# Five matmuls for a K tile instead of six, softplus on VectorE, and first casts in a written order

## The chip, the cores and the metric

The kernel runs on one core of a Trainium2 chip. The metric is the time of one execution on the device in microseconds (us). Before the change it is 855.6 us, the median of three runs (855.42, 855.6 and 856.59). In the profile, PE is TensorE's matmul, PEld its weight load, DVE is VectorE, ACT is ScalarE, POOL is GpSimd, SP is SyncE, which issues most DMAs. L85 is line 85 of the kernel.

## The reference, cut to what matters

One layer for 512 prompt tokens and 64 sample tokens, which share the weights: together T = 576 tokens, D_MODEL = 1024, D_FF = 2816, all in float32.

```python
h = rmsnorm(x, norm_mix)
proj = einsum('bld,de->ble', h, w_in)        # columns for three groups of heads
# A, gated DeltaNet, 4 heads: conv + SiLU on q, k, v; chunks of 64 rows
g = -exp(a_log) * softplus(aa + a_dt_bias)
beta = sigmoid(ab)
o_a, new_delta = gated_delta_rule(q, k, v, g, beta, delta_s0)
# B, differential attention, 4 heads; C, trailing means of 4 channel groups
x = x + einsum('ble,ed->bld', concatenate([o_a, o_b, o_c]), w_out)
u = einsum('bld,df->blf', rmsnorm(x, norm_ffn), w_up)
gate, val = split_cols(causal_dwconv(u, buf, w_conv, b_conv), (D_FF, D_FF))
x = x + einsum('blf,fd->bld', silu(gate) * val, w_down)
y = rmsnorm(x, norm_final)
```

## The kernel before

Activations lie transposed: 128 channels on the partitions, 576 tokens along the free axis, so a product of 1024 channels has 8 K tiles of 128. To keep float32's accuracy on faster fp32r matmuls, weights and activations are split into a high part, rounded to fp32r, and a low part, the rest. A K tile of a product is wh·xh + wh·xl + wl·xh, and each of the three goes in two matmuls, over the tokens 0 to 255 and 256 to 575 (`PARTS`): six matmuls, each with its own weight load, 1728 columns.

`gemm` (L190) makes one tile of 128 output channels in a PSUM tile `g` of 1024 columns (two banks), of which there are two. The tokens lie in its columns 256 to 831, so that the first part ends one bank and the second begins the other; columns 0 to 255 are unused. `accumulate` does a share of the K tiles of such a product. Each product takes its weights from `weights`: one 128x1024 slab at a time is loaded by SP (`w_raw`), cast on ACT (L174, `w_hi`) and subtracted on VectorE (L175, `w_lo`), two buffers each, so the next slab's cast waits until TensorE has read the buffer of the one before.

The order of the work on TensorE is written out: `mm` and `transpose` keep their instructions in program order and move a clock on by the columns at 2.4 GHz. Side work (the chains of the heads, the decay, the convolutions, the transposes of the result) are generators; `spawn` and `yield n` write their next matmuls n ns of that clock later, between the K tiles of the running product. On VectorE, ACT and POOL a scheduler sets the order. The program computes, in this order: the first two tiles of w_in together with the split of x (L340 to L368); 30 more tiles of w_in, beside which the delta rule and the attention run; w_out in 8 tiles, first 8 K tiles of each (the sum goes to DRAM, `x1_d`), then the other 4, which need the last heads of the attention (L1190 to L1202; the sum is read back as `w`, and the first two tiles of this part have their products begun early); ffn_up in 44 tiles, each with conv, SiLU and product; ffn_down in 8 tiles of 22 K tiles, whose sum `xr` (L1259) is transposed by TensorE (L89) and normed. The last tile of ffn_down has its own loop (`last_weights`, L1176).

The decay (`gates`) needs softplus: a chain of small operations of 128x20 elements, of which 17 run on POOL and the others on VectorE (L474 to L489), then `gt`, which four small matmuls read (they are written 11000 ns after the chain is issued).

Of the kernel before, what the change touches and what calls it, by code (L numbers as in the profile page):

```python
# [26 lines left out]
PARTS = (slice(0, CUT), slice(CUT, T))  # L27
O0 = 512 - CUT
# [31 lines left out]
def hybrid_step(ctx: ExitStack, tc: tile.TileContext, I, O):  # L60
# [69 lines left out]
    def act_tile():  # L130
        return act.tile([P, T], F32R, name="a", bufs=NSLOT)
# [60 lines left out]

    def gemm(xs):
        ps = psg.tile([P, 1024], F32, name="g")
        n = 3 * len(xs)
        i = 0
        xs = iter(xs)
        while i < n:
            for wh, wl in weights():
                xh, xl = next(xs)  # L200
                for w, x in ((wh, xh), (wh, xl), (wl, xh)):
                    for r in PARTS:
                        mm(ps[:, O0:O1][:, r], w, x[:, r], start=i == 0, stop=i == n - 1)
# [56 lines left out]
    def col(nm, i):  # L260
        return par[:, off[nm] + i:off[nm] + i + 1]
# [10 lines left out]
    def wide_pair():  # L272
        return [act.tile([P, KT, T], F32R, name="wide", bufs=2) for _ in range(2)]

    hmix_hi, hmix_lo = wide_pair()
    hmix = [(hmix_hi[:, k], hmix_lo[:, k]) for k in range(KT)]

# [23 lines left out]
    load_first(nc.scalar, slice(0, 2))  # L301
    load_first(nc.sync, slice(2, 8))
# [32 lines left out]
    def first_products():  # L335
# [1017 lines left out]
```

## Time and profile before

| | before |
|---|---|
| median of three runs | 855.6 us |
| the profiled execution | 856.47 us |
| its span, first to last instruction | 854.7 us |
| PE busy | 835.0 us (98%), 6350 matmuls |
| VectorE busy | 534.3 us (63%) |
| ACT busy | 357.3 us (42%) |
| POOL busy | 116.1 us (14%) |
| mean granted clock of TensorE | 0.991 |

The profiled execution is 0.9 us over the median, and 1.8 us of it lie outside the span. A share of busy time is a mean over stages that have different limits, so it only tells where to look; a wait of TensorE is told by the engine and line that released it. Where operations on one line are pipelined, the distance from one start to the next tells their cost, not their listed length.

### The profile page before, as it was taken

The page shows a single profiled execution, that of the slowest core. Times are in us where ns is not written, and L with a number is a line of the kernel's source. Part 1 is how long each engine was busy: PE and PEld are TensorE (multiplying, and loading weights), DVE is VectorE, ACT ScalarE, POOL GpSimd, SP SyncE. Part 2 cuts the span into 40 slices and gives each one's busy share as a digit, 9 for nine tenths or more (in the row PEclk, how much of TensorE's full clock was granted, in tenths as well). Part 3 has the DMA queues.
Part 4 walks back from the last instruction along what each step waited for, and adds up shares of the span by engine and source line. Part 5 has one row for each costly group of instructions (what it writes and reads, how often), then busy time and mean ns, then how long its engine had stood idle before and what let it go on. Part 6 is the DMA issues. An engine that isn't in the chain of part 4 may idle for free.

```text
span 854.7 us, 15955 instructions
## 1 busy us (share of the span) xinstructions
PE 835.0 (98%) x6350; PEld 809.0 (95%) x6350; DVE 534.3 (63%) x1189; ACT 357.3 (42%) x789; POOL 116.1 (14%) x183
## 2 busy tenths in 40 slices
PE   9969999999999999999999999999999999999996
PEld 8969999999999888889999999999999999999996
DVE  7748876884347677774867767667667673323422
ACT  6336563144444455552544344343343442222322
POOL 3332310210002000000012112112121120000001
PEclk9989999999999999999999999999999999999998
DMA  6232222242113432425822222222222223333413
GB/s 245 75 100 78 79 79 77 94 123 77 41 60 94 162 102 67 131 81 170 293 72 78 90 84 75 99 76 80 93 76 97 77 69 111 86 103 86 122 58 111
DMA packets 39033, 84.83 MB, mean 99 GB/s; under 512 B 9387, under 2 KB 14527, under 8 KB 38959
## 3 DMA queue, kind: packets, MB, share of 16 engines
q1 hardware_dynamic: 37870, 82.31, 30.1%
q10 hardware_dynamic: 1088, 1.51, 0.5%
q8 instruction: 50, 0.82, 0.4%
q14 instruction: 25, 0.20, 0.1%
HBM read 72.98 MB, written 10.82 MB: 98 GB/s over the span
## 4 chain that ended last, share of the span: by engine, by line
PE 89%; DVE 4%; DMA 2%; ACT 2%; POOL 1%; issue 1%; POOLq 0%; SPq 0%; DVEq 0%; ACTq 0%
PE g L85 75%; PE m L85 11%; PE m L89 3%; DVE w_lo L175 1%; DMA XT<-gsum_d 1%; ACT w_hi L174 0%; DMA inv<-kq 0%; DMA w<-x_d 0%; DMA x<-in_xT_dram 0%; POOL t L484 0%; POOL t L483 0%; POOL osc L267 0%; DVE oatt L991 0%; DMA Xc<-inv 0%; DVE stat L950 0%
## 5 line engine op out<-in xcount | busy, mean ns | idle before, releaser
L85 PE MATMUL g<-wide,w_hi 128*128 128x256 f32 x1472 | 267.4, 302 | 0.9 <-ACT w_hi L342 0.6
L85 PE MATMUL g<-t,w_hi 128*128 128x256 f32 (+1 forms) x1408 | 242.7, 294 | 0.0
L85 PEld LDWEIGHTS g<-wide,w_hi 128*128 128x128 f32 x1472 | 224.0, 191 | 4.6 <-issue 1.3
L85 PEld LDWEIGHTS g<-t,w_hi 128*128 128x128 f32 x1408 | 210.2, 188 | 0.0
L174 ACT CAST w_hi<-w_raw 128x1024 fp32r<-128x1024 f32 (+2 forms) x109 | 110.6, 1016 | 169.2 <-PE g L85 158.8
L85 PE MATMUL g<-wide,w_lo 128*128 128x256 f32 x736 | 161.7, 302 | 0.2 <-DVE w_lo L343 0.2
L175 DVE TENSOR_TENSOR w_lo<-w_raw,w_hi 128x1024 fp32r<-128x1024 f32 (+2 forms) x109 | 128.2, 1177 | 46.5 <-ACT w_hi L174 45.2
L85 PE MATMUL g<-t,w_lo 128*128 128x256 f32 x704 | 150.4, 295 | 0.0
L85 PEld LDWEIGHTS g<-wide,w_lo 128*128 128x128 f32 x736 | 124.2, 191 | 2.3 <-issue 0.9
L85 PEld LDWEIGHTS g<-t,w_lo 128*128 128x128 f32 x704 | 117.4, 188 | 0.1
L1215 POOL COPY fout<-u 128x4 f32<-128x4 f32 x44 | 51.2, 1164 | 223.1 <-DVE u L1206 223.1
L1212 DVE SCALAR_TENSOR_TENSOR c<-u,par,c 128x511 f32<-128x511 f32 (+3 forms) x176 | 78.9, 511 | 2.5 <-ACT c L1208 2.5
L1206 DVE TENSOR_TENSOR u<-g,rstd 128x576 f32<-128x576 f32 x44 | 33.3, 758 | 59.8 <-PE g L85 58.3
L85 PE MATMUL g<-w,w_hi 128*128 128x256 f32 (+1 forms) x280 | 48.4, 295 | 0.0
L85 PEld LDWEIGHTS g<-w,w_hi 128*128 128x128 f32 x280 | 42.0, 188 | 0.0
L1208 ACT ACTIVATE c<-u,par 128x576 f32<-128x576 f32 x44 | 38.3, 870 | 4.2 <-DVE u L1206 1.4
L1232 ACT ACTIVATE s<-c 128x576 f32<-128x576 f32 x22 | 15.1, 687 | 46.0 <-DVE c L1214 46.0
L267 POOL TENSOR_TENSOR osc<-sso,mhalf 128x5 f32<-128x5 f32 x8 | 9.4, 1182 | 179.6 <-DVE sso L772 62.3
L85 PE MATMUL g<-w,w_lo 128*128 128x256 f32 (+1 forms) x140 | 29.9, 294 | 0.0
L1143 ACT ACTIVATE junk<-m 128x128 f32<-128x128 f32 (+1 forms) x40 | 10.9, 274 | 43.7 <-PE m L89 35.3
L1144 DVE TENSOR_TENSOR t<-m,nf 128x128 f32<-128x128 f32 (+1 forms) x40 | 11.2, 289 | 23.7 <-ACT junk L1143 23.7
L85 PE MATMUL g<-kq,w_hi 128*128 128x256 f32 (+1 forms) x128 | 23.4, 301 | 0.0
(314 smaller groups left out, 1026.3 us busy)
## 6 DMA issues: line engine op xcount, KB each, us to landing
w_raw<-in_ffn_up_dram SPq DMA_DIRECT2D x44, 512.0 KB, 3.2
w_raw<-in_w_in_dram SPq DMA_DIRECT2D x30, 512.0 KB, 3.3
w_raw<-in_ffn_down_dram SPq DMA_DIRECT2D x16, 512.0 KB, 3.5
w_raw<-in_w_out_dram SPq DMA_DIRECT2D x8, 512.0 KB, 3.6
w_raw<-in_ffn_down_dram SPq DMA_DIRECT2D x8, 384.0 KB, 3.2
xr<-in_xT_dram SPq DMA_DIRECT2D x8, 288.0 KB, 3.5
x_d<-xr SPq DMA_DIRECT2D x8, 288.0 KB, 2.1
w<-x_d SPq DMA_DIRECT2D x8, 288.0 KB, 5.8
```

The source lines that it names most:

```text
L85: ordered(nc.tensor.matmul(out, lhsT=lhsT, rhs=rhs, start=start, stop=stop), n / 2.4 if rhs.dtype == F32R else max(54, n / 0.6))
L89: ordered(nc.tensor.transpose(out=out, in_=in_, identity=identity), 107)
L174: nc.scalar.copy(hi[:, :kt], raw)
L175: last_split[0] = nc.vector.tensor_sub(lo[:, :kt], raw, hi[:, :kt].bitcast(F32)).ins
L267: nc.gpsimd.tensor_tensor(out, x, epst[:x.shape[0], :x.shape[1]], op=ALU.pow)
L1143: nc.scalar.activation(junk[:n], src, AF.Square, scale=D ** -0.5, accum_out=op["part"][:n, c, m:m + 1])
L1144: nc.vector.tensor_mul(op["yt"][c][m // 4][:n, (m % 4) * P:(m % 4 + 1) * P], src, op["nf"][:n, m * P:(m + 1) * P])
L1206: nc.vector.tensor_mul(u, ps[:, O0:O1], rstd)
L1208: nc.scalar.activation(c, u, AF.Identity, scale=fw[:, 2, t:t + 1], bias=col("ffn_conv_b", t))
L1212: nc.vector.scalar_tensor_tensor(c[:, a + d:b], u[:, a:b - d], fw[:, j, t:t + 1], c[:, a + d:b], op0=ALU.mult, op1=ALU.add)
L1215: nc.gpsimd.tensor_copy(fout[:, :, :, t], u[:, NP - 64:].rearrange("p (s c) -> p s c", c=64)[:, :, 62:])
L1232: nc.scalar.activation(s, cv[0], AF.Silu)
```

## The change

A K tile becomes five matmuls. The high and the low part of an activation now lie in one tile, so that the 256 first tokens of both can stream through the same high weight at once: 512 columns, high part into the columns 256 to 511 of `g` as before, low part into the columns 0 to 255. `fold` adds the two when a product is complete: a copy to SBUF on ACT, an addition on VectorE. The tiles of activations become pairs (`act_pair`, `wide_pairs`, `t_pair`, `wide_slot`); the last tile of ffn_down keeps its six matmuls.

The softplus series runs on VectorE alone, and its matmuls are written 6500 ns after it instead of 11000. Three other delays grow. At the start, ACT's casts, activations and squares are kept in a written order, and the squares of a pair of channels come one step later.

```diff
+    def k_tile(ps, w, x, start=False, stop=False):
+        (wh, wl), (xh, xl, xb) = w, x
+        mm(ps[:, :2 * CUT].rearrange("p (a t) -> p a t", a=2), wh, xb, start=start, stop=False)
+        yield False
+        mm(ps[:, O0:O1][:, REST], wh, xh[:, REST], start=start, stop=False)
+        mm(ps[:, O0:O1][:, REST], wh, xl[:, REST], start=False, stop=False)
+        yield False
+        mm(ps[:, O0:O1][:, REST], wl, xh[:, REST], start=False, stop=stop)
+        mm(ps[:, O0:O1][:, HEAD], wl, xh[:, HEAD], start=False, stop=stop)
+        yield False
+
+    def fold(ps):
+        low = act.tile([P, CUT], F32, name="low", bufs=2)
+        nc.scalar.copy(low, ps[:, :CUT])
+        nc.vector.tensor_add(ps[:, O0:O1][:, HEAD], ps[:, O0:O1][:, HEAD], low)
+
     def gemm(xs):
         ps = psg.tile([P, 1024], F32, name="g")
-        n = 3 * len(xs)
         i = 0
-        xs = iter(xs)
-        while i < n:
-            for wh, wl in weights():
-                xh, xl = next(xs)
-                for w, x in ((wh, xh), (wh, xl), (wl, xh)):
-                    for r in PARTS:
-                        mm(ps[:, O0:O1][:, r], w, x[:, r], start=i == 0, stop=i == n - 1)
-                    i += 1
-                    yield False
+        while i < len(xs):
+            for w in weights():
+                yield from k_tile(ps, w, xs[i], i == 0, i == len(xs) - 1)
+                i += 1
+        fold(ps)
         return ps
...
+    nc.scalar.copy(epst[:, :1], epst[:, :1])
...
+        for j in range(KT // 2):
+            for k in (2 * j, 2 * j + 1):
...
+                tc.keep_in_program_order(nc.scalar.activation(hi, x, AF.Identity, scale=col("norm_mix", k)))
...
+                if k < 2:
+                    split_first((slice(0, 2), slice(2, 8))[k])
+                for w in range(2):
+                    for _ in k_tile(ps[w], (his[w][:, k], los[w][:, k]), hmix[k], k == 0, k == KT - 1):
+                        pass
+            if j:
+                add_squares(j - 1)
+        add_squares(KT // 2 - 1)
+        for p in ps:
+            fold(p)
...
-        nc.gpsimd.tensor_scalar_add(t2, t1, 2.0)
+        nc.vector.tensor_scalar_add(t2, t1, 2.0)
         nc.vector.reciprocal(t2, t2)
-        nc.gpsimd.tensor_mul(z, t1, t2)
-        nc.gpsimd.tensor_mul(z2, z, z)
-        nc.vector.tensor_scalar(t1, z2, 1.0 / 17, 1.0 / 15, op0=ALU.mult, op1=ALU.add)
-        for d in (13, 11, 9, 7, 5, 3, 1):
-            nc.gpsimd.tensor_mul(t1, t1, z2)
-            nc.gpsimd.tensor_scalar_add(t1, t1, 1.0 / d)
-        nc.vector.scalar_tensor_tensor(t1, t1, 2.0, z, op0=ALU.mult, op1=ALU.mult)
+        nc.vector.tensor_mul(z, t1, t2)
+        nc.vector.tensor_mul(z2, z, z)
+        nc.vector.tensor_scalar_mul(t1, z2, 1.0 / 17)
+        for d in (15, 13, 11, 9, 7, 5, 3):
+            nc.vector.scalar_tensor_tensor(t1, t1, 1.0 / d, z2, op0=ALU.add, op1=ALU.mult)
+        nc.vector.tensor_scalar(t1, t1, 1.0, 2.0, op0=ALU.add, op1=ALU.mult)
+        nc.vector.tensor_mul(t1, t1, z)
...
-        yield 11000
+        yield 6500
...
-            yield 1530
+            yield 2600
...
-            yield 1070
+            yield 1900
...
-                yield 400 + nk
+                yield 1000 + nk
```

On VectorE, before, around the softplus (`t_468` and `z` are its tiles, `tmp`, `vT` and `kq` belong to heads, `gt` is what TensorE waits for):

```order
L481 TENSOR_SCALAR t_468<-z_471 128x20
L175 TENSOR_TENSOR w_lo<-w_raw,w_hi 128x1024
L540 SCALAR_TENSOR_TENSOR vT<-tmp,ah,vT 128x579 x3
L545 SCALAR_TENSOR_TENSOR vT<-tmp,vT 128x579
L485 SCALAR_TENSOR_TENSOR t_468<-t_468,z 128x20
L535 TENSOR_TENSOR tmp<-g,rstd_129 128x512
L536 TENSOR_TENSOR tmp<-g,rstd_129 128x64
L486 SCALAR_TENSOR_TENSOR t_468<-y,t_468 128x20
L175 TENSOR_TENSOR w_lo<-w_raw,w_hi 128x1024
L489 SCALAR_TENSOR_TENSOR gt<-t_468,ea 128x20
L540 SCALAR_TENSOR_TENSOR kq<-tmp,ah,kq 128x579
L492 MEMSET gt 64x4
```

and after, where `t_454` is the series:

```order
L180 TENSOR_TENSOR w_lo<-w_raw,w_hi 128x1024
L498 TENSOR_SCALAR t_454<-z_457 128x20
L214 TENSOR_TENSOR g<-g,low 128x256
L500 SCALAR_TENSOR_TENSOR t_454<-t_454,z_457 128x20
L552 TENSOR_TENSOR tmp<-g,rstd_130 128x512
L553 TENSOR_TENSOR tmp<-g,rstd_130 128x64
L500 SCALAR_TENSOR_TENSOR t_454<-t_454,z_457 128x20 x5
L557 SCALAR_TENSOR_TENSOR vT<-tmp,ah,vT 128x579
L500 SCALAR_TENSOR_TENSOR t_454<-t_454,z_457 128x20
L557 SCALAR_TENSOR_TENSOR vT<-tmp,ah,vT 128x579
L501 TENSOR_SCALAR t_454<-t_454 128x20
L557 SCALAR_TENSOR_TENSOR vT<-tmp,ah,vT 128x579
```

The series now stands on VectorE itself, between one `w_lo`, a fold and the head's products; the second `w_lo` no longer stands before `gt`. On TensorE the `gt` matmuls stood behind K tile 32 and now stand behind K tile 30.

On VectorE, before, where the second part of w_out begins (the last `xr` of the first part, then the running sums `w`):

```order
L1099 TENSOR_TENSOR xr<-xr,g 128x576
L175 TENSOR_TENSOR w_lo<-w_raw,w_hi 128x512
L1131 MEMSET r_5141 128x5
L1252 MEMSET part 128x40
L1193 TENSOR_TENSOR w_4809<-w_4809,g 128x576
L1193 TENSOR_TENSOR w_4825<-w_4825,g 128x576
```

and after:

```order
L180 TENSOR_TENSOR w_lo<-w_raw,w_hi 128x512
L214 TENSOR_TENSOR g<-g,low 128x256
L1119 TENSOR_TENSOR xr<-xr,g 128x576
L1154 MEMSET r_4897 128x5
L1270 MEMSET part 128x40
L214 TENSOR_TENSOR g<-g,low 128x256
L1218 TENSOR_TENSOR w_4593<-w_4593,g 128x576
L214 TENSOR_TENSOR g<-g,low 128x256
L1218 TENSOR_TENSOR w_4593<-w_4593,g 128x576
```

`xr` has moved behind a `w_lo` and a fold, and each sum `w` behind a fold of its own.

On VectorE, before, at the end of one tile of ffn_down (`xr` is its sum, `t` the normed result after the transposes):

```order
L175 TENSOR_TENSOR w_lo<-w_raw,w_hi 128x768
L175 TENSOR_TENSOR w_lo<-w_raw,w_hi 128x1024
L1259 TENSOR_TENSOR xr<-xr,g 128x576
L175 TENSOR_TENSOR w_lo<-w_raw,w_hi 128x1024
L1144 TENSOR_TENSOR t<-m,nf 128x128 x4
L1144 TENSOR_TENSOR t<-m,nf 64x128
```

and after:

```order
L180 TENSOR_TENSOR w_lo<-w_raw,w_hi 128x768
L180 TENSOR_TENSOR w_lo<-w_raw,w_hi 128x1024 x2
L214 TENSOR_TENSOR g<-g,low 128x256
L1277 TENSOR_TENSOR xr<-xr,g 128x576
L1167 TENSOR_TENSOR t<-m,nf 128x128 x4
L1167 TENSOR_TENSOR t<-m,nf 64x128
```

The sum `xr` has moved behind the second `w_lo` of 1024 and a fold. On TensorE the transposes of `xr` stand as many K tiles behind the end of the product as before.

## Rows read from the trace of the kernel before

**Rows 1.** The page, busy us, share of the span and instructions of TensorE.

```profile
PE 835.0 (98%) x6350; PEld 809.0 (95%) x6350; DVE 534.3 (63%) x1189; ACT 357.3 (42%) x789; POOL 116.1 (14%) x183
```

**Rows 2.** TensorE's waits: line, releaser, us in total, times, longest.

```profile
PE m L85 <- ACT wt L970: 1.2, 3, 0.4
...
PE m L85 <- DVE Y L679: 0.8, 1, 0.8
```

**Rows 3.** Timeline of all engines around the decay, idle time and releaser in brackets.

```profile
37.57 1.05 ACT L174 CAST w_hi<-w_raw 128x1024 fp32r<-128x1024 f32 x1 [1.18 <-PE g L85]
...
37.84 0.69 DVE L535 TENSOR_TENSOR tmp<-g,rstd 128x512 f32<-128x512 f32 x1 [0.44 <-PE g L85]
...
39.79 2.53 DVE L540 SCALAR_TENSOR_TENSOR vT<-tmp,ah,vT 128x579 f32<-128x579 f32 x3
...
46.41 0.26 POOL L484 TENSOR_SCALAR t<-t 128x20 f32<-128x20 f32 x1
...
46.70 0.18 DVE L485 SCALAR_TENSOR_TENSOR t<-t,z 128x20 f32<-128x20 f32 x1 [2.78 <-POOL t L484]
...
49.92 1.01 PE L85 MATMUL m<-gt,cst 128*128 128x20 f32 x4 [5.73 <-DVE gt L492]
...
51.84 1.33 PE L85 MATMUL g<-wide,w_hi 128*128 128x256 f32 x4
```

**Rows 4.** Busy us by engine, TensorE's clock, DMA share, GB/s of a stretch.

```profile
191.22:194.63 3.41, 3.41 (x21) 3.13 (x20) 3.14 (x8) 2.87 (x10) 0.00 (x0) 0.52 0.00 0
```

**Rows 5.** TensorE's timeline in ffn_up: start, us, line, operation, tiles, count.

```profile
600.05 0.69 PE L85 MATMUL g<-t,w_hi 128*128 128x256 f32 x4
...
601.63 0.28 PE L85 MATMUL g<-t,w_hi 128*128 128x256 f32 x1
```

**Rows 6.** TensorE's timeline in the last ffn_down tile, same columns.

```profile
832.06 1.92 PE L85 MATMUL m<-wide,u 128*128 128x320 f32 x12
833.83 4.56 PE L85 MATMUL m<-w,t 128*128 128x320 f32 x30
838.22 1.34 PE L85 MATMUL m<-a,s 128*128 128x256 f32 x10
...
839.97 1.56 PE L85 MATMUL m<-wide,c 128*128 128x256 f32 x12
841.37 1.33 PE L85 MATMUL m<-wide,u 128*128 128x256 f32 x10
```

**Rows 7.** Timeline of VectorE in ffn_down, same columns.

```profile
738.56 1.23 DVE L175 TENSOR_TENSOR w_lo<-w_raw,w_hi 128x1024 fp32r<-128x1024 f32 x1
```

**Rows 8.** Timeline of ACT at the end of the first products.

```profile
21.12 1.99 ACT L174 CAST w_hi<-w_raw 128x1024 fp32r<-128x1024 f32 x2 [1.53 <-PE g L85]
```

**Rows 9.** Groups by line and shape: busy us, mean ns, idle before (ACT).

```profile
L927 ACT COPY wts<-m 128x256 f32<-128x256 f32 x4 | 1.5, 372 | 2.3 <-PE m L85 2.3
```

**Rows 10.** The same groups of VectorE.

```profile
L603 DVE SCALAR_TENSOR_TENSOR U<-m,w,tq 128x256 f32<-128x256 f32 x16 | 7.5, 478 | 0.9 <-PE m L85 0.7
...
L343 DVE TENSOR_TENSOR w_lo<-w_raw,w_hi 128x256 fp32r<-128x256 f32 x2 | 0.8, 418 | 0.0
```

**Rows 11.** Timeline where the second half of w_out begins.

```profile
395.13 0.62 ACT L174 CAST w_hi<-w_raw 128x512 fp32r<-128x512 f32 x1 [2.74 <-issue]
...
395.35 0.76 DVE L1099 TENSOR_TENSOR xr<-xr,g 128x576 f32<-128x576 f32 x1 [2.19 <-PE g L85]
...
401.92 0.80 PE L85 MATMUL g<-wide,w_hi 128*128 128x256 f32 x4 [0.21 <-DVE w L1193]
```

**Rows 12.** Groups of VectorE there, 402 to 422 us.

```profile
L1198 DVE SCALAR_TENSOR_TENSOR t<-w,par,t 128x576 fp32r<-128x576 f32 x7 | 5.7, 816 | 0.7 <-ACT t L1197 0.7
L1193 DVE TENSOR_TENSOR w<-w,g 128x576 f32<-128x576 f32 x7 | 5.3, 751 | 0.5 <-DMA w<-x_d 0.2
...
L175 DVE TENSOR_TENSOR w_lo<-w_raw,w_hi 128x512 fp32r<-128x512 f32 x4 | 2.7, 686 | 1.3 <-ACT w_hi L174 1.3
```

**Rows 13.** Timeline of TensorE in ffn_down.

```profile
740.48 0.71 PE L89 MATMUL m<-cst,xr 128*128 128x128 f32 x5
```

More of the change, by code (lines that the diff above doesn't have):

```diff
@@ L27 @@
 PARTS = (slice(0, CUT), slice(CUT, T))
+HEAD, REST = PARTS
 O0 = 512 - CUT
@@ L270, in hybrid_step, with wide_pairs @@
     x2_d = dram.tile([P, KT, T], F32, name="x2_d")
[L272 to L276, printed above, removed]
+    def wide_pairs():
+        tiles = [act.tile([P, KT // 2, 2, T], F32R, name="wide", bufs=2) for _ in range(2)]
+        return [split_pair(t[:, k]) for t in tiles for k in range(KT // 2)]
+    hmix = wide_pairs()
     abstack = ExitStack()
@@ L614, in hybrid_step @@
         last_inv = [None]
+        rows_pair = []
         def invert():
             n = 80
-            rows = [act_tile().bitcast(F32)[:n, :512] for _ in range(2)]
+            rows = [rows_pair[0][:n, i, :512] for i in range(2)]
             xb_f = kq_tile().rearrange("p i t -> p (i t)")[:n]
@@ L857, in attn_proj @@
             else:
-                dst = [act_tile().bitcast(F32) for _ in range(2)]
+                pair = act_pair().bitcast(F32)
+                dst = [pair[:, 0], pair[:, 1]]
             for i in range(3):
@@ L1036, in own_weight @@
             nc.sync.dma_start(raw, src)
-            hi, lo = (act_tile()[:, :512].rearrange("p (k m) -> p k m", m=P) for _ in range(2))
+            pair = act_pair()
+            hi, lo = (pair[:, i, :512].rearrange("p (k m) -> p k m", m=P) for i in range(2))
             nc.scalar.copy(hi, raw)
@@ L1073, in projections @@
             yield from after("windows")
-            his, los = wide_pair()
-            for i in range(8):
-                mixed[4 + i] = his[:, i], los[:, i]
+            mixed.update(zip(range(4, 12), wide_pairs()))
             yield from after("delta")
@@ L1164, in last_weights @@
         def last_weights():
-            tags = [("t", 16)] * 6 + [("u", 2)] * 2 + [("c", 3)] * 2 + [("s", 2)] * 2
+            halves = [t[:, i] for t in (t_pair(), t_pair(), t_pair()) for i in range(2)]
+            halves += [fp.tile([P, T], F32R, name=nm, bufs=bufs) for nm, bufs in (("u", 2), ("c", 3), ("s", 2)) for _ in range(2)]
             ws = []
@@ L1173, in last_weights @@
                     n = min(4, kt - b)
-                    hi, lo = (fp.tile([P, T], F32R, name=nm, bufs=bufs)[:, :n * P].rearrange("p (k m) -> p k m", m=P)
-                              for nm, bufs in (tags.pop(), tags.pop()))
+                    hi, lo = (halves.pop()[:, :n * P].rearrange("p (k m) -> p k m", m=P) for _ in range(2))
                     nc.scalar.copy(hi, raw[:, b:b + n])
@@ L1247, in feed_forward @@
             nc.sync.dma_start(op["nf"], I["norm_final"].partition_broadcast(P))
-            op["yt"] = [[fp.tile([P, T], F32R, name="t", bufs=16).bitcast(F32)[:, :512] for _ in range(2)]
-                        for c in range(5)]
+            op["yt"] = [[t[:, i, :512] for i in range(2)] for t in (t_pair().bitcast(F32) for c in range(5))]
             op["part"] = fin.tile([P, 5, KT], F32, name="part")
```

93 lines of the change are left out of this document (40 added, 53 removed).

## The prediction, made before the changed kernel had run

> **What bounds the kernel now.** I read the page's busy times first: TensorE is busy 98% of the span [rows 1]. The end is therefore set by how long the matrix products take and by the few places where TensorE stands still. The second view is TensorE's own waits: the reader is to see how small they are, 1.2 us in 3 for `wt` and 0.8 us for `Y` [rows 2], beside a single large one of 5.73 us for the decay `gt`, which the timeline shows in its place [rows 3]. The third is a table of stretches, for the granted clock: it fell to 0.52, about 1.2 GHz, from 191.22 on, in the 3.41 us behind a stretch in which TensorE had waited for `Y` [rows 4]. Last come the products themselves, in TensorE's timeline.
>
> **Five matmuls for six.** A K tile takes (601.63 - 600.05)/2 = 0.79 us [rows 5]. It streams 3 x (256 + 320) = 1728 columns, at 2.4 GHz 0.72 us; 70 ns are over, or 11.7 ns per matmul. After the change it streams the same 1728 columns in five matmuls: two of 256 become one of 512, so one weight load and one matmul's excess go. No matmul of 512 columns of this kind stands in the trace. The nearest rows are runs of one shape near the end: 12 of 320 columns take 833.83 - 832.06, 147.5 ns each (14.2 over 320/2.4); 30 of 320 take 146.3 ns (13.0 over); 12 of 256 take 841.37 - 839.97, 116.7 ns (10.0 over) [rows 6]. If the excess belongs to the matmul, 512 columns take 213.3 + 10.0 to 14.2 = 223.3 to 227.5 ns against 2 x 116.7 = 233.4, a gain of 5.9 to 10.1 ns. If it belongs to the columns, 512 take 233.4 and nothing is gained; a straight line through 116.7 and 147.5 gives even 239.9, a loss of 6.5 ns. I take the excess of the longest run of the shape nearest to 512, 13.0 ns: 226.3 ns, gain 7.1 ns. There are 858 K tiles (w_in 256, w_out 96, ffn_up 352, ffn_down 7 x 22 = 154; the last ffn_down tile keeps its six). 858 x 7.1 ns = **-6.1 us** (ends +5.6 and -8.7). TensorE waits for nothing in those stretches, so this is on the path. VectorE, ACT and the weight DMAs have as much to do per gemm as before, in 8 x 7 ns less, apart from the fold below.
>
> The Trainium skill (TensorE: Matmul & The Clock Gate, "Wait — 56ns, not 53.3ns?") speaks against part of this gain: it says that back to back a matmul costs its columns at 2.4 GHz plus a fixed part of about 2.5 ns. By it one matmul less per K tile saves 858 x 2.5 = 2.1 us instead of 6.1, and the sum below would be 4.0 us higher. The rows do not agree on the total (10 to 14 ns over, not 2.5), but they do not show how much of it is fixed.
>
> **Softplus on VectorE.** Before, TensorE reaches the `gt` matmuls at 49.92 - 5.73 = 44.19 and stands until 49.92; the POOL series of 14 operations ends only at 46.41 + 0.26, and VectorE then still has `tmp`, a `w_lo` and `gt` itself to do [rows 3]. After, the gt matmuls are written behind K tile 30 instead of 32, so TensorE comes 2 x 0.79 = 1.6 us earlier, at about 42.6. The order on VectorE puts a `w_lo` into the chain whose cast ends at 37.57 + 1.05 = 38.62 [rows 3]; from there: `w_lo` 1.23 [rows 7], a fold 0.42, `tmp` 0.69 and its small second part, about 0.9 together, three `vT` products 2.53 [rows 3], and 13 small operations of 20 columns or fewer (up to 0.18 each [rows 3]) about 2.0: 38.6 + 1.2 + 0.4 + 0.9 + 2.5 + 2.0, about 45.6. TensorE waits some 3.1 to 3.4 us instead of 5.73: -2.4. Behind the old wait four matmuls took 1.33 us instead of 0.69, at half clock [rows 3, 5]; about two K tiles ran so, 1.6 to 1.9 us. A wait of 3 us may bring that again; I count a quarter of it as won, -0.4. Together **-2.8 us** (0 if chain and clock stay; -7.6 if both go). The series leaves POOL; nobody then waits for POOL here but the next `cout` copies, which are not on the path. VectorE's new small operations stand before products `kq`, whose reader is the ACT and then the transposes; the wait for `kt` behind them I leave as it is.
>
> **Longer delays** (front tokens 2600, levels 1900, values 1000 + nk). They write the waiting matmuls later among K tiles that need nothing: the `wt` waits (1.2) and the `Y` wait (0.8) go [rows 2], and with the latter perhaps the half clock: 3.41 us at 0.52 did work of 1.77 us [rows 4], so 1.6 us hang on it; I count half. **-2.8 us** (-1 to -3.7). What is late next is the end of the inversion's six levels, which then comes later by 6 x 0.8 us; the head work that waits for it has gemms of other heads beside it.
>
> **Start.** The first products are bound by the hi and lo parts, as before. In VectorE's new order the last `total` addition stands behind the `w_lo` of the third weight, whose cast waits for the first buffers, that is for TensorE's K tile 16; before, it ran at 21.12 to 23.11 with the next one [rows 8] and nothing of the sums stood behind it. The first products end about 1 us sooner, the sums start about 2 us later than they could: **+0.7 us** (-1 to +3).
>
> **The fold.** Each of the 99 gemms gets an ACT copy 128x256 out of PSUM and a VectorE addition 128x256 in PSUM before its result can be read. Nearest rows: ACT 372 ns; VectorE 418 ns without and 478 ns with PSUM [rows 9, 10]; I take 0.37 and 0.42. In most stages the gemm's result is used several us before anyone needs it, and 99 x 0.42 = 42 us of VectorE lie beside TensorE. In three places they don't.
>
> First, the second half of w_out (8 gemms of 4 K tiles). Before, the last `xr` addition starts at 395.35 and the x1 store and loads follow it; TensorE has products of the first two tiles to do meanwhile and then meets its data 0.21 us late, at 401.92 [rows 11]. After, VectorE's order has `w_lo` (whose cast ends at 395.13 + 0.62), fold and then `xr`: 395.75 + 0.69 + 0.42 + 0.76 = 397.6 instead of 396.1, +1.5 us with no cover. From there each gemm gives VectorE 0.82 + 0.75 + 0.69 and a squares addition like the second, 3.0 us [rows 12], against 4 x 0.79 = 3.16 of TensorE; with 0.42 it is 3.4 against 3.13, and two PSUM buffers tie one to the other: 7 x 0.29 = 2.0. **+3.5 us** (1 to 5).
>
> Second, ffn_down. The transposes of `xr` stand 3.67 K tiles (2.9 us) behind the gemm's end in both orders, since their delay of 2500 is kept. Before, VectorE added `xr` at once, while ACT still cast, then did `w_lo` at 738.56, when the cast had ended; the transposes came at 740.48, with no wait [rows 7, 13]. After, the order is `w_lo`, fold, `xr`: 738.56 + 1.23 + 0.42 + 0.76 = 740.97, that is 0.65 us after the transposes' weight load is due at about 740.34. Five tiles at 0.65 and one, where the last weights' splits stand there too, at 1.5: **+4.8 us** (2 to 6). ffn_up has the same order, but its reader comes a whole gemm later.
>
> Third, the heads' chains, queued behind `w_lo` and fold: **+0.5 us** (0 to 4).
>
> **Sum.** -6.1 - 2.8 - 2.8 + 0.7 + 3.5 + 4.8 + 0.5 = -2.2 us. The profiled execution took 856.47 us, its span 854.7 and 1.8 around it; so 852.5 and 854.3. The median of the three runs is 855.6, 0.9 under the profiled one, and on its scale I forecast **853.4 us**.
>
> **Rivals.**
> (A) The excess is per column. For it: the excess grows from 10.0 to 14.2 when the columns grow by a quarter [rows 6]. Against: it grows by less between 256 and the run of 30. The gain of 6.1 is then nothing: 859.5, slower. It decides from 512 columns taking over about 231 ns. The Trainium skill's small fixed part (the section above) leads to the same side, with 857.4.
> (B) VectorE's place in the order decides: `w_lo`, fold and `xr` end more than 2.9 us behind a gemm's end, and each 0.1 us over that costs 0.1 in six ffn_down tiles and about as much in seven w_out gemms. If the ACT copy, queued behind a cast, and the addition come in a row (0.8 instead of 0.42), it is 6 x 0.4 + 7 x 0.6 = +6.6: 860.0, slower. For it: ACT's order has the copy behind the next cast. Against: that cast ends before `w_lo` does, so the copy is done when VectorE comes to it.
> (C) The waits go wholly: no gt wait and no half clock (-7.6 instead of -2.8), and in ffn_down VectorE takes 2.0 instead of 4.8. 853.4 - 4.8 - 2.8 = 845.8. For it: 13 small operations are short on VectorE. Against: `w_lo` and fold stand among them.
> (D) The change does not do this part: `gt` is as late as before against its matmuls and the clock falls again. 853.4 + 2.8 = 856.2.
>
> **Chances.** What a measurement of this kernel can tell from no change is about 0.2%, 1.7 us: faster is under 853.9, slower over 857.3. Forecast 0.42 (own range 849 to 857.5): of it 0.27 faster, 0.11 same, 0.04 slower. A 0.20: 0.03, 0.05, 0.12. B 0.12: 0, 0.02, 0.10. C 0.16: all faster. D 0.10: 0.02, 0.06, 0.02. Together 0.48, 0.24, 0.28. The range goes from C to just over B, 845 to 861; what it leaves out is A with a loss per matmul (865) and C with more.
>
> **What would show it.** Pitch of a K tile in ffn_up: 0.783 us if right, 0.79 with A, 0.78 or under with a larger gain. The `gt` wait about 3.3 us and at 42 us instead of 44. TensorE waits for `xr` in six ffn_down tiles, 0.6 each; none would make me wrong by 4.8. A TensorE wait of over 1 us at the start of w_out's second half. Waits for `wt` and `Y` gone. Wrong altogether: the five matmuls slower than six, or waits that I have nowhere, as for folds in ffn_up.

## The result, and the profile after

The changed kernel takes 888.6 us (median of 4 runs, 887.9 to 890.1) against 856.1 us: ratio 1.038, 95% interval 1.036 to 1.040. The forecast was 853.4 us, so it is 35 us off and on the wrong side, outside the range of 845 to 861. The profiled execution took 888.5 us with a span of 886.7, 32.0 more than before.

The page of the changed kernel first: busy us of the engines, and TensorE's granted clock in 40 slices, in tenths of full speed.

```profile
PE 845.2 (95%) x5492; PEld 775.3 (87%) x5492; DVE 569.0 (64%) x1299; ACT 378.6 (43%) x889; POOL 52.1 (6%) x166
...
PEclk9999999999999999789999999999999999999998
```

Line numbers are those of the changed kernel (`mm` is L86 there, the cast L179, `w_lo` L180, the fold L213 and L214). TensorE has 858 matmuls fewer than in [rows 1], one per K tile, and is busy 10 us longer; it stands still for 41.5 us instead of 19.7. Slices 17 and 18 (354 to 399 us) have a clock of 0.7 and 0.8. The waits of TensorE are the second view (line, releaser, us in total, times, longest):

```profile
PE m L90 <- DVE p L978: 4.5, 3, 2.6
PE m L90 <- DVE xr L1277: 3.1, 6, 1.3
PE m L86 <- DVE gt L509: 3.0, 1, 3.0
PE m L86 <- DVE wide L1018: 2.7, 2, 1.4
PE m L90 <- DVE m L967: 2.4, 2, 1.6
PE g L86 <- DVE w L1218: 2.3, 3, 1.0
PE m L90 <- ACT p L972: 2.0, 1, 2.0
PE m L86 <- DVE total L367: 2.0, 1, 2.0
```

`wt` and `Y` of [rows 2] are gone. `gt` has fallen from 5.73 to 3.0 us, and the stretch at half clock that comes with it, by the granted clock, from 6.8 to 3.4 us. In their place stand `p`, `m` and `wide`: they belong to the softmax and the output of the attention, which had 0.5 us of such waits before, and the prediction had 0.5 us for them. `xr` (ffn_down), `w` (w_out's second part) and `total` (the start) are the ones it named.

To see where the 32.0 us are, I counted the columns of the products in both traces; the time at which the same K tile begins can then be compared, whatever stands between. Each row is the change of the time of a stretch:

| K tiles | what runs there | before | after | change |
|---|---|---|---|---|
| to 16 | start, first two products | 29.8 | 31.9 | +2.2 |
| 16 to 64 | w_in, decay (`gt`) | 55.9 | 51.2 | -4.7 |
| 64 to 128 | w_in, fronts of the heads | 60.0 | 62.9 | +2.9 |
| 128 to 256 | w_in, inversion, delta rule | 152.1 | 152.3 | +0.2 |
| 256 to 304 | first part of w_out, attention | 82.4 | 107.4 | +25.0 |
| 304 to 352 | rest of it, second part | 41.1 | 44.5 | +3.4 |
| 352 to 704 | ffn_up | 280.7 | 280.3 | -0.4 |
| 704 to the end | ffn_down, output | 152.7 | 156.2 | +3.4 |

**The products.** In ffn_up nothing but the products decides. TensorE's timeline of the changed kernel, with single matmuls' starts (start, us, engine, line, operation, tiles, count):

```profile
600.45 0.40 PE L86 MATMUL g<-t,w_hi 128*128 128x512 f32 x1
...
600.68 0.46 PE L86 MATMUL g<-t,w_hi 128*128 128x320 f32 x2
...
600.98 0.43 PE L86 MATMUL g<-t,w_lo 128*128 128x320 f32 x2
...
601.24 0.39 PE L86 MATMUL g<-t,w_hi 128*128 128x512 f32 x1
```

The 512 columns take 600.68 - 600.45 = 0.23 us, the two of 320 take 0.30, the 320 and the 256 take 0.26: 0.79 us again, as in [rows 5]. Over all K tiles from 600 to 700 us the distance from a matmul of 512 to the next is 230.9 ns on average; two of 256 took 2 x 116.7 = 233.4 in [rows 6], 2.5 ns more. ffn_up's 352 K tiles gained 0.4 us, 1.1 ns each. The rate is not the same everywhere: K tiles 128 to 176, where TensorE ran nothing but products, took 38.40 us before and 38.08 after, 6.7 ns less per K tile.

**The attention.** The busy times of the heads' stretches, two before (first fence) and three after (busy us of PE, PEld, DVE, ACT, POOL with counts, then TensorE's clock, DMA share, GB/s):

```profile
313.00:328.00 15.00, 14.59 (x106) 12.11 (x105) 10.47 (x37) 8.72 (x25) 0.00 (x0) 1.00 0.22 75
340.00:354.00 14.00, 14.00 (x105) 12.03 (x105) 10.00 (x33) 7.88 (x24) 0.00 (x0) 1.00 0.24 82
```

```profile
317.00:338.00 21.00, 17.73 (x95) 14.02 (x94) 12.05 (x41) 8.95 (x29) 1.17 (x1) 0.84 0.17 54
351.00:372.00 21.00, 18.06 (x93) 14.76 (x92) 11.34 (x38) 7.61 (x23) 0.00 (x0) 0.76 0.16 53
386.00:406.00 20.00, 17.82 (x97) 14.17 (x96) 12.23 (x42) 8.87 (x26) 0.19 (x1) 0.83 0.18 57
```

No engine is near its limit after. TensorE stands idle 3.3, 2.9 and 2.2 us in the three stretches, and in each of them the clock is at 1.2 GHz for part of the time: 0.84, 0.76 and 0.83 on average, that is 2 x (1 - 0.84) x 21 = 6.7 us, 10.1 and 6.8 us at half clock. At full clock the work of these 23.6 us takes half, so 11.8 us go with the clock. TensorE's waits in the whole attention sum up to 13.1 us (1.7 before). 13.1 - 1.7 + 11.8 = 23.2 of the 25.0.

Here is the first of the stretches, with a piece of the head before it, in TensorE's timeline of the changed kernel:

```profile
299.31 1.09 PE L86 MATMUL m<-cv,wts 128*64 128x128 f32 x8
...
316.19 1.13 PE L86 MATMUL m<-kq 64*128 64x512 f32 x4
...
322.45 1.33 PE L86 MATMUL m<-ew,pr 128*128 128x64 f32 x10 [1.25 <-DVE ew L936]
...
325.02 0.66 PE L90 MATMUL m<-cst,p 128*128 128x128 f32 x4
327.69 0.92 PE L90 MATMUL m<-cst,oatt 128*128 128x128 f32 x5 [2.02 <-ACT p L972]
328.54 1.97 PE L86 MATMUL m<-cv,wts 128*64 128x128 f32 x8
...
332.78 1.31 PE L86 MATMUL g<-wide,w_hi 128*128 128x512 f32 x3
```

The widest scores (`m<-kq`, 64x512) run at 316.19. TensorE then waits 1.25 us for `ew`, and 2.02 us at 327.69, where a PSUM bank is freed by the exponentials of the next scores. Behind that the eight matmuls `m<-cv,wts` take 1.97 us, where the same eight took 1.09 us for the head before, at 299.31: the clock has fallen. What VectorE did between the scores and their maximum, in the changed kernel:

```profile
317.11 1.23 DVE L180 TENSOR_TENSOR w_lo<-w_raw,w_hi 128x1024 fp32r<-128x1024 f32 x1 [1.16 <-ACT w_hi L179]
...
318.38 0.45 DVE L214 TENSOR_TENSOR g<-g,low 128x256 f32<-128x256 f32 x1
...
318.83 0.62 DVE L968 TENSOR_REDUCE stat<-m 128x1 f32<-128x512 f32 x1
...
319.43 0.74 DVE L1119 TENSOR_TENSOR xr<-xr,g 128x576 f32<-128x576 f32 x1
320.10 0.68 DVE L968 TENSOR_REDUCE stat<-m 128x1 f32<-128x512 f32 x1
...
320.77 1.04 DVE L1009 TENSOR_SCALAR oatt<-oatt,osc 128x128 f32<-128x128 f32 x5
321.73 0.22 DVE L969 TENSOR_SCALAR stat<-stat,qneg 128x2 f32<-128x2 f32 x1
...
322.05 0.26 DVE L936 TENSOR_SCALAR ew<-cst,mx 128x64 f32<-128x64 f32 x1
```

VectorE idles 1.16 us for a cast, because `w_lo` stands first; then come a fold, one maximum (`stat`), `xr`, the other maximum, the five `oatt`. The scaled maximum, for which the exponentials wait, is ready at 321.73 + 0.22 = 321.95, 5.8 us after the scores began. Before, the order was the maxima and `xr` first and `w_lo` behind them (both engines' timeline of the kernel before):

```profile
310.08 1.13 PE L85 MATMUL m<-kq 64*128 64x512 f32 x4
...
312.29 0.67 DVE L950 TENSOR_REDUCE stat<-m 128x1 f32<-128x512 f32 x1
...
313.88 0.75 DVE L1099 TENSOR_TENSOR xr<-xr,g 128x576 f32<-128x576 f32 x1
314.54 0.23 DVE L951 TENSOR_SCALAR stat<-stat,qneg 128x2 f32<-128x2 f32 x1
314.67 1.22 DVE L175 TENSOR_TENSOR w_lo<-w_raw,w_hi 128x1024 fp32r<-128x1024 f32 x1
```

There it took 314.77 - 310.08 = 4.7 us. For the next head the scaled maximum of the changed kernel is ready at 356.44 + 0.21 = 356.65, 6.8 us after the scores, and TensorE waits for `m`, and later for `p`, both from VectorE:

```profile
349.89 1.13 PE L86 MATMUL m<-a 64*128 64x512 f32 x4
...
356.44 0.21 DVE L969 TENSOR_SCALAR stat<-stat,qneg 128x2 f32<-128x2 f32 x1
...
360.37 1.09 PE L90 MATMUL m<-cst,p 128*128 128x128 f32 x4 [1.59 <-DVE m L967]
...
380.63 0.30 PE L90 MATMUL m<-cst,p 128*128 128x128 f32 x1 [2.60 <-DVE p L978]
```

In the order on TensorE the widest scores of heads 1 to 3 stood at K tiles 262, 278 and 294 before and stand at 264, 280 and 296 after. All these products have 8 K tiles and begin at multiples of 8, so the scores have moved to the very place where a product ends and `w_lo`, fold and `xr` come due.

### The profile page after: what moved, and what is told of

It is laid out like the page before. It is cut to its first block, busy times and chain, and to the rows that moved or that the text cites. A ratio compares the mean times of both kernels' runs of the same rounds, so it can differ in the third digit from the quotient of the medians.

```text
span 886.7 us, 14467 instructions
## 1 busy us (share of the span) xinstructions
PE 845.2 (95%) x5492; PEld 775.3 (87%) x5492; DVE 569.0 (64%) x1299; ACT 378.6 (43%) x889; POOL 52.1 (6%) x166
## 4 chain that ended last, share of the span: by engine, by line
PE 81%; DVE 9%; ACT 4%; DMA 3%; issue 2%; ACTq 0%; POOLq 0%; SPq 0%; DVEq 0%
PE g L86 67%; PE m L86 12%; PE m L90 2%; DVE w_lo L180 2%; ACT w_hi L179 2%; DVE stat L968 1%; DMA w_raw<-in_ffn_down_dram 1%; DVE g L214 1%; ACT p L972 1%; DMA w_raw<-in_w_out_dram 1%; DMA w_raw<-in_w_in_dram 1%; DMA XT<-gsum_d 1%; DVE xr L1277 1%; DMA inv<-kq 0%; DVE w L1218 0%
## 5 line engine op out<-in xcount | busy, mean ns | idle before, releaser
L86 PE MATMUL g<-wide,w_hi 128*128 128x512 f32 x1104 | 269.1, 350 | 2.8 <-DVE w L1218 1.4
L86 PE MATMUL g<-t,w_hi 128*128 128x320 f32 (+1 forms) x1056 | 241.3, 337 | 0.8 <-DVE w L1218 0.8
L86 PEld LDWEIGHTS g<-wide,w_hi 128*128 128x128 f32 x1104 | 186.1, 192 | 21.2 <-DVE wide L374 1.6
L180 DVE TENSOR_TENSOR w_lo<-w_raw,w_hi 128x1024 fp32r<-128x1024 f32 (+2 forms) x109 | 128.3, 1177 | 104.6 <-ACT w_hi L179 104.0
L179 ACT CAST w_hi<-w_raw 128x1024 fp32r<-128x1024 f32 (+2 forms) x109 | 110.3, 1012 | 192.7 <-PE g L86 183.1
L86 PEld LDWEIGHTS g<-t,w_hi 128*128 128x128 f32 x1056 | 174.2, 188 | 15.7 <-issue 1.0
L86 PE MATMUL g<-wide,w_lo 128*128 128x320 f32 x736 | 160.6, 300 | 0.0
L86 PE MATMUL g<-t,w_lo 128*128 128x320 f32 x704 | 150.8, 295 | 0.0
L86 PEld LDWEIGHTS g<-wide,w_lo 128*128 128x128 f32 x736 | 125.3, 192 | 1.3 <-issue 0.9
L86 PEld LDWEIGHTS g<-t,w_lo 128*128 128x128 f32 x704 | 117.0, 188 | 0.1
L214 DVE TENSOR_TENSOR g<-g,low 128x256 f32<-128x256 f32 x99 | 42.1, 425 | 12.4 <-ACT low L213 12.3
L86 PE MATMUL g<-w,w_hi 128*128 128x320 f32 (+1 forms) x210 | 48.1, 337 | 0.0
L213 ACT COPY low<-g 128x256 f32<-128x256 f32 x99 | 36.3, 367 | 14.4 <-PE g L86 14.4
L86 PEld LDWEIGHTS g<-w,w_hi 128*128 128x128 f32 x210 | 34.6, 188 | 3.0
L86 PE MATMUL g<-w,w_lo 128*128 128x320 f32 (+1 forms) x140 | 29.9, 295 | 0.0
L1239 POOL COPY fout<-u 128x4 f32<-128x4 f32 x44 | 8.4, 190 | 266.8 <-DVE u L1230 266.8
L86 PE MATMUL g<-kq,w_hi 128*128 128x320 f32 (+1 forms) x96 | 23.9, 352 | 0.0
```

The costliest lines, as they stand in the source:

```text
L86: ordered(nc.tensor.matmul(out, lhsT=lhsT, rhs=rhs, start=start, stop=stop), n / 2.4 if rhs.dtype == F32R else max(54, n / 0.6))
L179: nc.scalar.copy(hi[:, :kt], raw)
L180: last_split[0] = nc.vector.tensor_sub(lo[:, :kt], raw, hi[:, :kt].bitcast(F32)).ins
L213: nc.scalar.copy(low, ps[:, :CUT])
L214: nc.vector.tensor_add(ps[:, O0:O1][:, HEAD], ps[:, O0:O1][:, HEAD], low)
```

## The experiments

Theories, as they stood one after the other. V: the longer delays themselves cost, by holding PSUM banks. F: the folds cost. P: the place of the attention's chain against the ends of the products decides what the fold costs. O: within F, not the fold's work but the order that the scheduler gives it (`w_lo` ahead of fold and `xr`). The times of whole runs are medians; waits and stretches of K tiles are those of the one profiled execution of each run. K tiles 256 to 304 are called the attention (82.4 us before, 107.4 after).

**1. One delay undone** (`e1_values400`)

```diff
-                yield 1000 + nk
+                yield 400 + nk
```

> The changed kernel with one number undone: the attention's value matmuls are written 400 + nk ns after their transposes again, not 1000 + nk. Theory V (the longer value delay holds PSUM banks longer, so that the next scores and their chain to the transposed p come late): K tiles 256 to 304, which lost 25 us against the kernel before, lose under 8, and the time is about 870. Theory F (w_lo and fold stand on VectorE ahead of the softmax chain of each head): the 25 us stay, 884 to 892; perhaps 1 us more, since the waits for wt come back.

886.1 us; the attention takes 102.0 us. V's form for this delay falls: 5 us of the attention, not 17.

**2. All three delays undone** (`e2_delays`): 1530, 1070 and 400 + nk.

> The changed kernel with all three longer delays undone (front tokens 1530, levels 1070, values 400 + nk). Theory V: about 868. Theory F: 885 to 893, the waits for Y and wt back (2 to 3 us) and the loss in K tiles 224 to 232 (5.7 us) unchanged. If that loss goes, it came from the delays of the levels or of the front.

868.8 us, and the attention takes 86.1. Neither theory had it so: V was right in the time, though the value delay alone did little. The order shows what the front and level delays do there, since they end long before: with them short, the widest scores stand at 262.3, 278 and 294 again. That gave theory P.

**3. Six matmuls and no fold, with all else of the change** (`e3_six`): `k_tile` does the six matmuls of before, `fold` does nothing.

> The changed kernel with six matmuls for a K tile and no fold (but for the last tile, as before), everything else of the change kept. Theory F: the 25 us of the attention go, and those of the second half of w_out (2.8) and of ffn_down (3.1) too: 852 to 858. Theory V: about 880, only w_out and ffn_down regain.

860.5 us (ratio 1.002, interval 1.000 to 1.004); the attention takes 91.1. So the new place and the longer delays cost 9 us even without folds, and folds and five matmuls the other 16. The time is a little over what F gave.

**4. Five matmuls, folds and the start's order only** (`e4_five_only`): softplus and delays of before.

> The changed kernel with softplus on POOL again (11000) and the three delays of before: five matmuls, folds and the order of the start are left of the change. Theory F: 886 to 894 (the attention loses its 25 us all the same, and the gt wait of 5.7 us is back). Theory V: about 870.

874.0 us, attention 86.2: F fails here too, as in run 2. Against run 2, which differs in the softplus and its delay alone, softplus on VectorE is worth 5.2 us here, of it 1.7 in K tiles 16 to 64 and 3.0 in K tiles 176 to 200.

**5 and 6. The place moved, with nothing else** (`e5_phase`, `e6_after_shift`): one delay of the second head is longer by 1450 ns, in run 5 with the three old delays, in run 6 with the new ones.

```diff
-                yield 920
+                yield 920 + (1450 if h == 1 else 0)
```

> The changed kernel with the three old delays (the run of 868.8 us), and in it one delay of the attention's second head longer by 1450 ns, so that the widest scores of heads 1 to 3 are written at K tiles 264.3, 280 and 296 (the end of a product of 8 K tiles) as in the changed kernel, not at 262.3, 278 and 294. Theory P (place): what costs is that the softmax chain then queues on VectorE behind w_lo, fold and the xr addition of that product's end; K tiles 256 to 304 take 100 us or more instead of 86.1, with TensorE waits for p, m, ew and a fall of the clock: 880 to 888 us. Theory V (the longer delays cost by themselves, through PSUM banks held longer): nothing moves, 867 to 871.

> The changed kernel with all its long delays, and that same delay of the second head longer by 1450 ns: the widest scores stand at K tiles 266, 282 and 298, two behind a product's end. Theory P: the chain comes behind w_lo, fold and xr instead of queueing at them; K tiles 256 to 304 lose under 10 us against before instead of 25, and the time is 868 to 876, up to 2 us of it for the last head's chain ending 2 K tiles later. Theory V: 886 to 891.

Run 5: 884.8 us, the median of two executions of 881.6 and 888.1. In the first of them, the profiled one, the attention takes 98.3, 12 us more than without the shift (a little under the 100 expected), with 5.5 us of waits for `p`. Run 6: 875.0 us, attention 89.9, 17.5 us less than the changed kernel. Scores at the end of a product cost most; two K tiles before it the attention loses 3.7 us against the kernel before, two behind it 7.5. P is shown from both sides.

V is not at nothing, though. With the scores at the product's end the attention takes 98.3 us with the old delays (run 5), 102.0 with two of them long (run 1) and 107.4 with all three. If the other execution of run 5 lost its 6.5 us there, it is 104.8 against 107.4, so the delays' own share lies between about 3 and 9 us. How they cost, by PSUM banks or otherwise, is not shown.

**7. No fold** (`e9_nofold`): `fold` is empty, the five matmuls, their order and all delays stay (the low part is missing from the result).

> The changed kernel without its fold: the ACT copy and the VectorE addition of each product are left out, so the low part of the first 256 tokens times the high weights is missing from the result. Order on TensorE, places and delays are those of the changed kernel. If the fold is what makes the chain late at that place: 856 to 862, w_out's second half and ffn_down regain their 2.8 and 3.1 us, and the attention loses about 9 as with six matmuls. If five matmuls themselves (their grouping between the side work) cost: 875 to 885.

856.4 us (ratio 1.000, interval 0.9985 to 1.0017); the attention takes 89.3, ffn_down and the output regain all of their 3.4 us, K tiles 176 to 200 take 29.9 us instead of 34.5. The folds are worth 32 us; the 6.9 us that the attention still loses against the kernel before are made up by gains elsewhere (3.4 us in K tiles 16 to 64, 3.5 in 176 to 200). Scores, VectorE and TensorE in its timeline, at the same place:

```profile
308.86 1.13 PE L86 MATMUL m<-kq 64*128 64x512 f32 x4
...
308.97 0.76 DVE L1117 TENSOR_TENSOR xr<-xr,g 128x576 f32<-128x576 f32 x1 [0.34 <-PE g L86]
309.78 1.23 DVE L180 TENSOR_TENSOR w_lo<-w_raw,w_hi 128x1024 fp32r<-128x1024 f32 x1
...
311.31 1.28 DVE L966 TENSOR_REDUCE stat<-m 128x1 f32<-128x512 f32 x2
...
312.95 0.22 DVE L967 TENSOR_SCALAR stat<-stat,qneg 128x2 f32<-128x2 f32 x1
...
319.38 1.41 PE L90 MATMUL m<-cst,oatt 128*128 128x128 f32 x5 [2.02 <-ACT p L970]
320.72 1.97 PE L86 MATMUL m<-cv,wts 128*64 128x128 f32 x8
```

`xr` fills the time of the cast, `w_lo` follows almost without idling, and the scaled maximum is ready 313.17 - 308.86 = 4.3 us after the scores. The wait of 2.02 us, and the eight slow matmuls behind it, stand here as in the changed kernel: they belong to the place and the delays, not to the fold. What goes with the folds are waits of the later heads for VectorE, 4.3 us for `p` and 2.4 for `m`, 1.5 of the 2.7 for `wide`, and nearly all of the wait for `ew`; the half clock of the attention falls from 23.9 to 3.4 us.

**8 and 9. Half a fold** (`e11_copy_only`, `e12_add_only`)

```diff
-        nc.vector.tensor_add(ps[:, O0:O1][:, HEAD], ps[:, O0:O1][:, HEAD], low)
```

is run 8; run 9 drops ACT's copy and adds a constant tile instead of `low`.

> The changed kernel whose fold keeps the ACT copy of the low part and leaves out VectorE's addition (the low part of the first 256 tokens is missing from the result). If VectorE's part of the fold (0.42 us in order, and its wait) is what delays the softmax chain, xr in ffn_down and the sums of w_out: 856 to 863. If ACT's copy, queued in front of the exponentials, is: 875 to 888.

> The changed kernel whose fold keeps VectorE's addition, but adds a constant tile instead of the low part, with no ACT copy (the low part is missing from the result). If VectorE's time and place in the order decide: 876 to 888. If it is the wait for ACT's copy, that is the two engines in a row: 858 to 868.

Copy only: 879.0 us, attention 102.2. Addition only: 872.7 us, attention 91.9. Both expectations on VectorE's part fail: most of the attention's loss comes with the copy on ACT (12.9 us over run 7, the addition 2.6), though VectorE then has no more to do than without a fold. The addition alone still costs 16.3 us in all, 6.2 of it in K tiles 176 to 200 and 2.0 at the start; the 22.6 us of the copy include 5.9 us in K tiles 176 to 200 and 3.3 in ffn_up. VectorE's order has changed all the same (timeline of run 8):

```profile
314.94 1.13 PE L86 MATMUL m<-kq 64*128 64x512 f32 x4
...
315.86 1.23 DVE L180 TENSOR_TENSOR w_lo<-w_raw,w_hi 128x1024 fp32r<-128x1024 f32 x1 [1.16 <-ACT w_hi L179]
...
317.14 0.73 DVE L1118 TENSOR_TENSOR xr<-xr,g 128x576 f32<-128x576 f32 x1
...
318.52 0.67 DVE L967 TENSOR_REDUCE stat<-m 128x1 f32<-128x512 f32 x1
...
320.16 0.21 DVE L968 TENSOR_SCALAR stat<-stat,qneg 128x2 f32<-128x2 f32 x1
```

`w_lo` waits 1.16 us for the cast and stands ahead of `xr`; the scaled maximum comes 320.37 - 314.94 = 5.4 us after the scores. In ffn_down either half alone costs nothing (K tiles 704 to 836 in 107.6 and 107.2 us, 107.8 before), both together 2.2 us.

**10 to 13. The order at a product's end written out** (`e13_ordered`, `e14_ordered_short` in the whole program; `e15_ordered_part`, `e16_ordered_part_short` only in the first part of w_out and in ffn_down; the short ones have the old delays).

```diff
-        nc.scalar.copy(low, ps[:, :CUT])
+        tc.keep_in_program_order(nc.scalar.copy(low, ps[:, :CUT]))
```

and likewise for the cast of `w_hi`, `w_lo`, the fold's addition and the three additions to `xr`.

> The changed kernel, with the end of a product kept in the written order on each engine: on ACT the fold's copy before the next cast, on VectorE the fold's addition and the xr addition before the next w_lo (in the changed kernel w_lo, fold, xr). Work, long delays and the attention's place are unchanged. Theory O (the order: w_lo, which waits for its cast, holds the fold, xr and the softmax chain up): the waits for xr in ffn_down (3.1 us) go, K tiles 256 to 304 take under 97 us instead of 107.4: 868 to 877. Theory T (the time and the two engines in a row of the fold itself, wherever it stands): 883 to 890.

> The same written order at a product's end, with the three old delays (the run of 868.8 us). Theory O: ffn_down regains 3 to 4 us, w_out's second half about 1.5, the attention 2 to 3: 859 to 863. Theory T: 867 to 870. If it were under 854, five matmuls would be worth keeping; expected not, since a K tile gains only 1.7 ns.

930.1 and 922.1 us. The written order holds casts back, above all in ffn_up (318.3 us instead of 280.3), and TensorE waits for weights: in run 10 29.5 us for `w_hi` and 16.4 for `w_lo`. The test was spoilt outside the stages in question, so it was confined:

> The changed kernel with its long delays; the written order at a product's end (fold's copy before the next cast on ACT, fold and xr before the next w_lo on VectorE) only in the first part of w_out, beside which the attention runs, and in ffn_down; elsewhere the order is the scheduler's. Theory O: no waits for weights in ffn_up, the xr waits of ffn_down (3.1 us) fall to about 1, and K tiles 256 to 304 take 97 to 101 us instead of 107.4: 877 to 881. Theory T: 885 to 890, with only the xr waits gone.

> The same partly written order with the three old delays (868.8 us without it). Theory O: ffn_down gains about 2 to 3 us, the attention at the old place 0 to 2: 864 to 867. Theory T: 867 to 870.

883.3 us, between the two theories, and 871.4, over both. The `xr` waits of ffn_down fall from 3.1 to 1.2 and 1.4 us, as O expected, though the stretch gains only 1 us. The attention gains 5.9 us at the new place (101.5) and loses 4.6 at the old one (90.7): O is at most a part there. Which of the order, ACT's copy and the added time does how much in the attention stays open.

**14. Six matmuls only beside the attention** (`e18_six_in_wout`): a flag makes `k_tile` and `fold` those of run 3 in the first part of w_out.

> The changed kernel, with six matmuls and no fold only in the first part of w_out (8 products, beside which the attention runs); five matmuls and fold everywhere else, all delays and places as changed. If the folds of just these products make the attention late: K tiles 256 to 304 take 89 to 92 us instead of 107.4, 870 to 874 in all. If the lateness is carried over from the stages before them: 880 to 888.

873.4 us, attention 91.2, in the range expected if the folds of just these products make the attention late. Five matmuls and the fold in these eight products cost the attention 16.2 us; the lateness is not carried in from the stages before.

**15 to 18. The other parts alone.** `e8_start_only` is the changed kernel with six matmuls, no fold, and softplus and delays of before; `e7_soft_only` and `e17_soft_k32` are the kernel before with softplus on VectorE, with a delay of 6500 and of 11000; `e10_soft_levels` is the first of these with 1500 for the levels and 900 ns less for the second head.

> The changed kernel with six matmuls and no fold, softplus on POOL and the three old delays: left are the order of the start and the activations in pairs. The place of the attention is that of before. Between runs K tile 16 starts 2.4 to 2.9 us later wherever that order stands, while the first matmul starts 2 us sooner; so 857 to 859, about 2 us slower than before. Rival: the late sums are made good by the gt wait behind them, 855 to 857.

859.4 us, ratio 1.0023 (1.0007 to 1.0038): a little slower and just over the expected range; K tile 16 begins 2.1 us later, and TensorE waits 2.0 us for `total`.

> The kernel before with one part of the change: softplus on VectorE, its matmuls written 6500 ns behind it instead of 11000. Between the two runs that differ in this alone (868.8 and 874.0) it was worth 5.2 us. Expected 850 to 853, faster than before: the gt wait falls from 5.7 to 3 us or less, and the half clock behind it goes or shortens. Rival: the gain depends on the start order of the change, 855 to 857.

854.1 us, ratio 0.9975 (0.9959 to 0.9991): 2 us faster than the kernel before, though 1 us over the expectation. The `gt` wait is still 3.2 us and the half clock behind it remains (6.8 us, as before).

> The kernel before with softplus on VectorE and the delay of 11000 kept, so that the gt matmuls stand behind K tile 32 as before and not 30. With 6500 gt was ready at 45.6 and TensorE came at 42.5, waited 3.2 us and then ran four matmuls at half clock; two K tiles later it should wait about 1.6 us, perhaps without the fall of the clock: 850 to 853.5. Rival: wait and half clock trade places with the kt transposes behind them, 853.5 to 855.

855.3 us, ratio 0.9986 (0.9975 to 0.9996), an interval that overlaps that of `e7_soft_only`. The wait is not shorter but longer; TensorE's timeline of that run:

```profile
49.23 1.01 PE L85 MATMUL m<-gt,cst 128*128 128x20 f32 x4 [5.19 <-DVE gt L492]
```

With the later place the scheduler put the series among the next head's products on VectorE, and `gt` came at 49.1 instead of 45.6. The small operations are the same in both runs; what differs is what stands between them on VectorE.

> The kernel before (six matmuls, its start) with softplus on VectorE (6500) and the levels of the inversion written 1500 ns apart instead of 1070; the second head's delay is 900 ns shorter, so that the widest scores stay at K tiles 262, 278 and 294. Expected: the wait for Y (1.1 us) and the half clock behind it go (K tiles 176 to 200 in 30 us instead of 33.5), the attention stays at 82.4 us: 849 to 852. Rival: the later end of the inversion stops TensorE as much in K tiles 200 to 232, 853 to 856.

856.3 us, ratio 0.9995 (0.9982 to 1.0008): against the kernel before, K tiles 176 to 200 gain 2.4 us, and 200 to 304 give 3.6 back. The rival held in what it said, though the loss reaches into the attention (2.0 us) and the time is just over its range.

## Why the prediction was wrong, step by step

**The heads' chains, +0.5 us (0 to 4): measured +25.0, and +2.9 in K tiles 64 to 128.** This is the step that failed. I priced the fold at 0.42 us of VectorE (it took 0.425) and looked for the readers that come soon after a product's end, in w_out's second part and ffn_down. The 0.5 us for the heads' chains had no row behind them: I did not lay the attention's own chain (scores, maximum, exponential, transposes) beside the ends of the products, although the order of the changed kernel shows that the widest scores moved there. Three things meet, by the profiled executions. The folds cost 3.7 us at the old place (86.1 against 82.4). The move to a product's end, where they stand, costs 12.2 more (98.3, run 5). The longer delays at that place bring it to 107.4, 9.1 more, though by the spread of run 5 it may be as little as 2.6. Without folds the new place and the delays cost 6.9 us (89.3). About half of the 25.0 us went with the fallen clock. Rival B had the mechanism, `w_lo` and fold ahead of what TensorE needs, with the wrong victim and 6.6 us as its price.

**Five matmuls, -6.1 us: measured -0.4 in ffn_up's 352 K tiles; in all between 1 and 4 us, as an estimate.** Against the 7.1 ns per K tile of the sum stand 1.1 ns in ffn_up, which would be 1 us in all, and 6.7 ns in K tiles 128 to 176. Runs 3 and 7 differ in five or six matmuls alone: 860.5 against 856.4 us is 4.1 us, but by their ratios to the kernel before (1.0022 and 1.0001) it is 1.8, and their intervals overlap. The excess over the columns' time grows with the columns for the most part: 10.0 ns at 256, 13.0 to 14.2 at 320, 230.9 - 213.3 = 17.6 at 512. In ffn_up rival A (no gain) was nearer than the sum, with 230.9 ns just under its limit of about 231. The run of 30 matmuls that I took as the nearest row said the opposite of what the slope between 256 and 320 said. The Trainium skill (TensorE: Matmul & The Clock Gate, "Wait — 56ns, not 53.3ns?") gives a fixed part of about 2.5 ns per matmul, by which one matmul less per K tile saves an estimated 2.1 us. That lies within what the runs allow: ffn_up gained less per K tile than these 2.5 ns, K tiles 128 to 176 more.

**Softplus, -2.8 us.** The wait fell to 3.0 us, as worked out (3.1 to 3.4). The half clock that comes with it was shorter too, 3.4 us instead of 6.8, and K tiles 16 to 64 gained 4.7 us in all, more than the sum. Alone on the kernel before, the part gave 2.0 us, with the half clock as long as before.

**Longer delays, -2.8 us.** `wt` and `Y` went, as said, but K tiles 176 to 200 took 1.0 us more; the 3.5 us that the delays give there (run 7) need a kernel without folds. The step left out that a delay moves everything that is written after it.

**Start, +0.7 us (-1 to 3): +2.2.** The mechanism is the one named, the last `total` behind a `w_lo`; the wait is 2.0 us. The sum did not have the clock, which fell behind that wait (0.62 on average from 24.0 to 28.5 us) and had not fallen there before.

**w_out's second part, +3.5: +3.4,** of it 2.3 us in three waits for `w`, 1.0 at its beginning. **ffn_down, +4.8 (2 to 6): +3.4 to the end,** with six waits for `xr`, 3.1 us in all and 1.3 the longest; run 7 shows that they are the fold's.

## What to carry to other kernels

Before a small operation is added at the end of every product, list what else comes due at that place on the same engines, over all stages, and look above all for chains from TensorE back to TensorE; a delay that moves such a chain is part of the same question. Merging two matmuls gains what the trace shows to be fixed per matmul, so fit two sizes, in more than one stage, before pricing it. Where a scheduler sets the order, read the order of the changed program at the places with the least slack, since an operation on one engine (here a copy on ACT) can change the order on another.

## What the runs showed of the hardware that I had not expected

A matmul of 512 columns with its own weight load took 230.9 ns from start to start in ffn_up, against 233.4 for two of 256: the cost over 2.4 GHz grew nearly with the columns (10.0, 13 to 14, 17.6 ns). And short waits came with stretches at half clock, though not in a fixed proportion: in the attention of the changed kernel TensorE stood idle for 13.1 us and ran 23.9 us at 1.2 GHz, which is some 12 us more than at full clock; in run 12 it stood idle for 12.9 us and ran 10.2 us at 1.2 GHz, and in run 6 4.2 us of idle time came with none.
